# Moving the norm's roots to GpSimd's DMA queue and four reordering copies to ScalarE, in the first stage of a two-layer decoder trunk

## The chip, the cores and the metric

The kernel runs on one NeuronCore of a Trainium2 chip, in one launch. The metric is the device time of one execution in microseconds (us). A core has TensorE (PE: matmuls and transposes), VectorE (DVE), ScalarE (ACT), GpSimd (POOL) and SyncE (SP), each of which runs its own list of instructions in order. A DMA is an instruction of the engine on whose queue it is put (here SP or POOL); if it has to wait for its data or its buffer, everything behind it on that engine waits too.

## The reference

```python
h = x                                        # (1, 512, 1024) float32
# layer 0: dilated attention, 3 groups of 4 heads, then a gated FFN with a short convolution
g = norm_gains[0]
qkv = rms_norm(h, g[0]) @ w_qkv_a[0]         # rms_norm: x * rsqrt(mean(x*x) + eps) * gain
# group g of ((128,1), (512,4), (2048,16)): (window, dilation); rope on q and k;
# with dilation r the tokens are taken as t.reshape(L, r).T, so every r-th token is a sequence
...
h = h + rms_norm(mix, g[1])
h = h + rms_norm(conv_ffn(rms_norm(h, g[2]), ...), g[3])
# layer 1: forgetting attention with shared K/V, then the same kind of FFN
```

The change lies in the very first stage: the norm of x, its product with w_qkv_a, and the layout of the tokens for the dilated groups. The rest (about nine tenths of the time) is untouched.

## The kernel before

All products are done in three matmuls of split operands: a float32 array is held as a rounded high part and the remainder, the low part, and `mm3` (lines 287 to 290) adds high x high, high x low and low x high. So every activation and every weight must be split first: ScalarE writes the high part, VectorE subtracts to get the low part.

**Weights.** The class `Weights` (line 33) holds a list of pieces of 512 KB each, in the order of use. Its methods are called in the order in which the program text says so: `load` puts a piece's DMAs on SP's queue (line 48), `high` splits on ScalarE (line 62, with the norm's gain as scale), `low` on VectorE (line 80). `W.split(n)` splits all pieces up to n and loads a few pieces ahead of that; `W.get()` hands out the next pair and splits up to `W.ahead - 1` pieces beyond it. Pieces 0 to 3 are q and k of group 0, pieces 4 and 5 its v; 6 to 9 are q and k of group 1, 10 to 13 of group 2, 14 to 17 v of both. The first six pieces go into buffers called wearly, the later ones into wraw.

**The roots.** The norm's factor 1/sqrt(mean) is not applied to x. x is transposed and split as it is, and the factor is applied to each output row when a product leaves PSUM. `rstd0(b)` computes it for token block b (128 tokens): ScalarE squares and sums (1146), takes the root (1147), VectorE the reciprocal (1148), into `rt[:, 0, b]`. For the dilated groups the tokens are in another order, so the same 512 numbers are needed in that order: `factors_out` (1150) writes `rt[:, 0]` to a small DRAM tile `rd` (1151) and reads it back as `rt[:, 1]` (1152), both on SP's queue. The read-back waits for the write.

**The second token order.** `xT` holds the transposed x, in high and low part, each in two halves (i = 0, 1) of four 128-row chunks (kc 0 to 3 and 4 to 7). Groups 1 and 2 use a copy `xP`, in which the tokens stand as (r, l) instead of (l, r), with r = 4. `reorder` (1160) makes it: for each half, block and part one GpSimd copy of 128 x 512 (1167). Every block of 128 columns of `xP` holds tokens from all four blocks of `xT`.

**The order of the stage**, as written by hand from line 1375 on:

- q and k of group 0 for blocks 0 to 3 (`qk0`), with the transposes and splits of the blocks and the pieces between them. `qk_post` (1174) takes each result out of PSUM on ScalarE with the factor (1178), and applies the rope on GpSimd (1184 to 1187).
- After block 1's `qk_post`: `reorder(0, 1)` on GpSimd (8 copies), `rstd0(2)`, `rstd0(3)`, `factors_out()`.
- After block 3's: the first loads of `down_sums` for pair (1,6) on SP (576: it loads two chunks of a w_down, forms four sums on VectorE and writes them to DRAM for a later stage), then `reorder(2, 3)` (8 copies).
- `v_proj0` (1316): v of group 0. Its two `W.get()` split pieces 6 and 7, then 8, before anything else of it. Blocks 0 and 1 are computed, taken out on ScalarE (1331), and the list `between[0]` is run; then blocks 2 and 3 and `between[1]`. In those lists stand the transposes of q and k (`qk_transpose`: TensorE 1193, the copy out on VectorE 1196), the first scores and their softmax (TensorE 1218, VectorE 1203, ScalarE 1204), and steps of the down sums.
- `wide_proj(1, ...)` (1426): q and k of group 1 from `xP`, in four weight steps s of two chunks kc, over all four blocks in each step. Steps 0 and 1 read the half i = 0, steps 2 and 3 the half i = 1. In step 3 `qk_post(1, b)` applies `rt[:, 1]`. Then `wide_proj(2, ...)` in the same way, and v of groups 1 and 2.

Buffers come from pools with a fixed number of slots (16 large ones, 10 small ones, 8 PSUM banks); an allocation waits until the last user of a freed slot is done.

Of the kernel before, what the change touches and what calls it, by code (L numbers as in the profile page):

```python
# [9 lines left out]
F32 = mybir.dt.float32  # L10
# [105 lines left out]
def trunk_kernel(ctx, tc, x, norm_gains, w_qkv_a, w_o_a, w_q_b, w_o_b, kv_norm, w_kvf, b_f,  # L116
                 w_up, conv_w, conv_b, w_down, rope, out):
    nc = tc.nc
    act, dve, pool, pe, sp = nc.scalar, nc.vector, nc.gpsimd, nc.tensor, nc.sync
# [11 lines left out]
    def t4(shape, dt=F32, name="t4"):  # L131
        return p4.tile(shape, dt, tag="t4", name=name)
# [4 lines left out]
    def bank(shape, name="bank"):  # L137
        return psp.tile(shape, F32, tag="ps", name=name)
# [16 lines left out]
    for g in range(3):  # L155
        for s in range(4):
            def f(raw, g=g, s=s):
                v = raw.rearrange("p (k t c) -> p k t c", k=2, t=2)
                src = wqkv.rearrange("(k p) (t c) -> p k t c", p=128, c=256)
                return [(v[:, k], src[:, 2 * s + k, g:g + 4:3, :]) for k in range(2)]  # L160
# [126 lines left out]
    def mm3(o, ah, al, bh, bl, first, last, shared=False):  # L287
        pe.matmul(o, ah, bh, start=first, stop=False, skip_group_check=shared)  # L288
        pe.matmul(o, ah, bl, start=False, stop=False, skip_group_check=shared)  # L289
        pe.matmul(o, al, bh, start=False, stop=last, skip_group_check=shared)  # L290
# [285 lines left out]
    def down_sums(pairs, place, queue, lag, behind):  # L576


        live, n = [], len(pairs)
        for i in range(n + lag + behind):  # L580
            if i < n:
                l, j = pairs[i]
                a, b = place()
                live.append((a, b))
                r = w_down[l][j * 256:j * 256 + 256, :].rearrange("(c p) d -> c p d", p=128)
                sp.dma_start(a, r[0])
                sp.dma_start(b[:, 0:512], r[1, :, 512:1024])
                sp.dma_start(b[:, 512:1024], r[1, :, 0:512])
            if 0 <= i - lag < n:
                a, b = live[i - lag]  # L590
                dve.tensor_tensor(a[:, 0:512], a[:, 512:1024], a[:, 0:512], ALU.subtract)
                dve.tensor_tensor(a[:, 512:1024], b[:, 0:512], a[:, 512:1024], ALU.subtract)
                dve.tensor_tensor(b[:, 0:512], b[:, 0:512], a[:, 0:512], ALU.subtract)
                dve.tensor_tensor(b[:, 512:1024], b[:, 512:1024], b[:, 0:512], ALU.subtract)
            i -= lag + behind
            if i >= 0:
                l, j = pairs[i]
                for q, t in enumerate(live[i]):
                    queue.dma_start(dT[l][j, :, q * 1024:q * 1024 + 1024], t)
            yield  # L600
# [539 lines left out]
    rt = sml.tile([128, 2, 4], F32, tag="rt", name="rt", bufs=1)  # L1140
    rd = tc.dram_tile([T], F32, name="rd")

    def rstd0(b):
        ss, sd = small(1, "s1"), small(1, "sd")
        junk = t2([128, D], BF16, name="junk")
        act.activation(junk, h[:, b, :], AF.Square, scale=1.0 / 32, accum_out=ss)
        act.activation(sd, ss, AF.Sqrt, bias=eps_t)
        dve.reciprocal(rt[:, 0, b:b + 1], sd)

    def factors_out():  # L1150
        sp.dma_start(rd.rearrange("(b p) -> p b", p=128), rt[:, 0])
        sp.dma_start(rt[:, 1], rd.rearrange("(l r) -> l r", r=4))

    def factor(g, b):
        return rt[:, min(g, 1), b:b + 1]

    def by_fourth(a, spec="p k (l r) -> p k r l"):
        return a.rearrange(spec, r=4)

    def reorder(*blocks):  # L1160

        for i in range(2):
            for b in blocks:
                for part in range(2):
                    src = by_fourth(xT[part][i][:, :, b * 128:b * 128 + 128])
                    dst = xP[part][i].rearrange("p k (r l) -> p k r l", r=4)[:, :, :, b * 32:b * 32 + 32]
                    pool.tensor_copy(dst, src.bitcast(F32))

    def ax(g, b, kc):
        return xs(xP if g else xT, kc, slice(b * 128, b * 128 + 128))  # L1170
# [3 lines left out]
    def qk_post(g, b, o):  # L1174
        if b == 0:
            qks[g] = t8([128, 4, 8, HD], name=f"qk{g}")
        qk = qks[g][:, b]
        act.activation(qk.rearrange("p a d -> p (a d)"), o, AF.Identity, scale=factor(g, b))
        tu = t2([128, 2, 8, 16], name="tu")
        rb = 4 * min(g, 1) + b  # L1180
        c2 = rp[:, rb, None, 0:16].to_broadcast([128, 8, 16])
        s_lo = rp[:, rb, None, 16:24].to_broadcast([128, 8, 8])
        s_hi = rp[:, rb, None, 24:32].to_broadcast([128, 8, 8])
        pool.tensor_tensor(tu[:, 0], qk[:, :, 0:16], c2, ALU.mult)
        pool.tensor_tensor(tu[:, 1, :, 0:8], qk[:, :, 8:16], s_lo, ALU.mult)
        pool.tensor_tensor(tu[:, 1, :, 8:16], qk[:, :, 0:8], s_hi, ALU.mult)
        pool.tensor_tensor(qk[:, :, 0:16], tu[:, 0], tu[:, 1], ALU.add)
# [128 lines left out]
    def v_proj0(between):  # L1316
        banks = []
        ws = [[t.rearrange("p (k c) -> p k c", k=4) for t in W.get()] for _ in range(2)]
        for b in range(4):
            if b % 2 == 0:  # L1320
                banks.append(bank([128, 2, 256], name="v_ps"))
            for kc in range(KD):
                wh, wl = ws[kc // 4]
                ah, al = ax(0, b, kc)
                mm3(banks[b // 2][:, b % 2, :], ah, al, wh[:, kc % 4, :], wl[:, kc % 4, :],
                    kc == 0, kc == KD - 1)
            if b == 1:
                V[0] = t4([128, 4, 256], name="V0")
            if b % 2:
                for i in range(2):  # L1330
                    act.activation(V[0][:, b - 1 + i, :], banks[b // 2][:, i], AF.Identity, scale=factor(0, b - 1 + i))
                for f in between[b // 2]:
                    f()
# [4 lines left out]
    L = later  # L1338
# [68 lines left out]
                      same[:, None, :].to_broadcast([128, 32, 4]), ALU.add)  # L1407
    qk0(1, 6, 7)
    qk_post(0, 1, qk_banks[1])
    reorder(0, 1)  # L1410
    rstd0(2)
    rstd0(3)
    factors_out()
    qk0(2, *range(4))
    W.split(5)
# [5 lines left out]
    qk_post(0, 3, qk_banks[3])  # L1421
    sums = down_sums([(1, 6), (1, 7)], in_two, sp, 1, 3)
    next(sums)
    reorder(2, 3)

    def wide_proj(g, name, post, between):

# [15 lines left out]
    def v_post(g, b, o):  # L1443
        if b == 0:
            for i in (1, 2):
# [2 lines left out]
        dve.tensor_scalar(V[2][:, b, :], o[:, 256:512], factor(2, b), None, ALU.mult)  # L1448

    down0 = down_sums([*[(0, j) for j in range(ND)], (1, 8)], in_one, sp, 1, 1)  # L1450
    v_proj0([[L(qk_transpose, 0, 0), L(qk_transpose, 0, 1), L(next, down0)],
             [L(qk_transpose, 0, 2), L(qk_transpose, 0, 3), L(scores, 0, 0), L(scores, 0, 1), L(next, sums), L(next, down0)]])
    wide_proj(1, "qk_ps", qk_post, [
        [L(p_transpose, 0, 0)],
# [352 lines left out]
    for n in range(N + 3):  # L1807
        live = n < N
        if live:
            j, i = units[n]  # L1810
# [93 lines left out]
```

## Time and profile before

| | us |
|---|---|
| median of 3 runs (lowest, highest) | 1109.35 (1109.13, 1109.38) |
| the profiled execution, its own time | 1110.01 |
| span of the profiled execution, first to last instruction | 1108.2 |
| TensorE busy / mean granted clock | 1095.6 (99%) / 0.996 |
| VectorE, ScalarE, GpSimd busy | 895.7, 730.9, 234.8 |
| DMA moved | 252.06 MB, 227 GB/s on average |

The profile shows one execution, instruction by instruction. In a timeline each row gives the start and length in us, the engine, the line of the kernel, the operation with its tiles (output <- inputs), and in brackets how long the engine stood idle before it and which instruction, or which DMA, ended that idle time. Rows with "q" after the engine's name (SPq) are DMA instructions on that engine's queue; their length is the issue and not the transfer. A list of waits sums such idle time by waiter and releaser. TensorE's granted clock is given as a share of full speed.

The stage of the change takes about the first 140 us. From 0 to 20 us TensorE is busy for 17.68 us, from 20 to 40 for 20.00, from 40 to 60 for 16.42 at a mean clock of 0.83, and from then on nearly without a gap at 1.00. The DMA engines' share is 0.80 in the first 20 us, 0.15 from 20 to 40, and about 1 from there to 120.

### The profile page before, as it was taken

What the parts mean: (1) busy time and instruction counts of PE and PEld (TensorE: products, weight loads), DVE (VectorE), ACT (ScalarE), POOL (GpSimd) and SP (SyncE); (2) the same over time, 40 slices, a digit from 0 to 9 for tenths busy, and PEclk for the clock granted to TensorE, in tenths of its full rate; (3) what the DMA queues carried; (4) which work ended last, traced back from release to release, by engine and by line L of the source; (5) the groups of instructions that cost most, each with busy time, mean ns of one, the idle gap of its engine ahead of it and who ended that gap; (6) DMA issues with size and microseconds to landing.
All of it is one profiled execution on the core that took longest, in us unless ns stands there. A gap on an engine that the chain in (4) does not pass through costs nothing. (4 is left out here: it accounts for less than half of the span.)

```text
span 1108.2 us, 18988 instructions
## 1 busy us (share of the span) xinstructions
PE 1095.6 (99%) x6905; PEld 970.1 (88%) x6905; DVE 895.7 (81%) x1453; ACT 730.9 (66%) x1228; POOL 234.8 (21%) x337
## 2 busy tenths in 40 slices
PE   9899999999999999999999999999999999999997
PEld 6788888999999988888878888888999999988886
DVE  5797788977887789997598777878977887789994
ACT  6454566677878757576563488846677878757572
POOL 2713100422222111000000545600422222211000
PEclk9899999999999999999999999999999999999999
DMA  5699963499999998884446756783499999999862
GB/s 195 243 354 404 367 194 99 96 228 228 235 223 238 225 297 314 324 314 123 133 152 232 244 153 158 224 269 97 96 227 233 236 217 245 222 296 315 321 247 76
DMA packets 156614, 252.06 MB, mean 227 GB/s; under 512 B 12960, under 2 KB 99992, under 8 KB 156520
## 3 DMA queue, kind: packets, MB, share of 16 engines
q1 hardware_dynamic: 138248, 186.61, 50.5%
q0 software_dynamic: 18272, 64.24, 26.2%
q8 instruction: 54, 0.88, 0.3%
q14 instruction: 40, 0.33, 0.1%
HBM read 166.08 MB, written 39.63 MB: 186 GB/s over the span
## 5 line engine op out<-in xcount | busy, mean ns | idle before, releaser
L288 PE MATMUL up<-xsh,w 128*128 128x256 f32 x512 | 144.9, 283 | 0.0
L289 PE MATMUL up<-xsl,w 128*128 128x256 f32 x512 | 144.9, 283 | 0.0
L290 PE MATMUL up<-xsh,w 128*128 128x256 f32 x512 | 144.9, 283 | 0.0
L288 PE MATMUL acc<-w 128*128 128x512 f32 (+1 forms) x311 | 120.7, 388 | 0.3 <-DVE mix L337 0.3
L290 PE MATMUL acc<-w 128*128 128x512 f32 (+1 forms) x311 | 120.6, 388 | 0.1
L705 ACT CAST w<-wraw 128x1024 fp32r<-128x1024 f32 x80 | 82.6, 1048 | 37.7 <-DVE wraw L689 37.7
L624 DVE SCALAR_TENSOR_TENSOR bb<-up,conv,bb 128x511 f32<-128x511 f32 x80 | 59.8, 747 | 57.2 <-ACT bb L623 57.0
L289 PE MATMUL acc<-w 128*128 128x512 f32 (+1 forms) x267 | 103.3, 387 | 0.0
L288 PEld LDWEIGHTS up<-xsh,w 128*128 128x128 f32 x512 | 98.3, 192 | 0.0
L289 PEld LDWEIGHTS up<-xsl,w 128*128 128x128 f32 x512 | 98.3, 192 | 0.0
L290 PEld LDWEIGHTS up<-xsh,w 128*128 128x128 f32 x512 | 98.3, 192 | 0.0
L623 ACT ACTIVATE bb<-up,conv 128x512 f32<-128x512 f32 x80 | 60.1, 778 | 32.7 <-DVE up L775 24.4
L288 PE MATMUL up<-xch,w 128*128 128x256 f32 (+1 forms) x256 | 80.0, 312 | 0.1
L288 PE MATMUL up<-xbh,w 128*128 128x256 f32 (+1 forms) x256 | 80.0, 312 | 0.1
L708 POOL DMA_DIRECT2D w<-wraw x48 | 41.0, 853 | 181.6 <-ACT w L707 102.9
L289 PE MATMUL up<-xcl,w 128*128 128x256 f32 (+1 forms) x256 | 79.2, 310 | 0.0
L289 PE MATMUL up<-xbl,w 128*128 128x256 f32 (+1 forms) x256 | 79.2, 310 | 0.0
L290 PE MATMUL up<-xbh,w 128*128 128x256 f32 (+1 forms) x256 | 79.2, 309 | 0.0
L290 PE MATMUL up<-xch,w 128*128 128x256 f32 (+1 forms) x256 | 79.2, 309 | 0.0
L76 DVE TENSOR_TENSOR w<-wraw,w 128x1024 fp32r<-128x1024 f32 x48 | 65.0, 1378 | 11.7 <-ACT w L58 11.2
L58 ACT CAST w<-wraw 128x1024 fp32r<-128x1024 f32 x62 | 63.8, 1052 | 15.6 <-PE v_ps L289 6.9
L290 PEld LDWEIGHTS acc<-w 128*128 128x128 f32 x311 | 58.4, 188 | 12.7 <-DVE w L817 0.9
(304 smaller groups left out, 3283.7 us busy)
## 6 DMA issues: line engine op xcount, KB each, us to landing
wraw<-in_w_up_dram SPq DMA_DIRECT2D x88, 512.0 KB, 7.0
w<-wraw POOLq DMA_DIRECT2D x62, 512.0 KB, 7.7
dT<-dsums SPq DMA_DIRECT2D x28, 512.0 KB, 6.9
dsums<-in_w_down_dram SPq DMA_DIRECT2D x22, 512.0 KB, 7.7
dsums<-in_w_down_dram SPq DMA_DIRECT2D x44, 256.0 KB, 6.9
hD<-hc POOLq DMA_DIRECT2D x44, 256.0 KB, 7.3
wraw<-dT SPq DMA_DIRECT2D x22, 512.0 KB, 7.0
dact<-hD SPq DMA_DIRECT2D x44, 256.0 KB, 5.4
```

The costliest lines, as they stand in the source:

```text
L58: self.nc.scalar.copy(pair[:, 0], raw)
L76: self.nc.vector.tensor_tensor(pair[:, 1], raw, pair[:, 0].bitcast(F32), ALU.subtract)
L288: pe.matmul(o, ah, bh, start=first, stop=False, skip_group_check=shared)
L289: pe.matmul(o, ah, bl, start=False, stop=False, skip_group_check=shared)
L290: pe.matmul(o, al, bh, start=False, stop=last, skip_group_check=shared)
L623: act.activation(bb[:, s, :], ps, AF.Identity, bias=cp[:, 3, ch:ch + 1], scale=cp[:, 2, ch:ch + 1])
L624: dve.scalar_tensor_tensor(bb[:, s, 1:], ps[:, :T - 1], cp[:, 1, ch:ch + 1], bb[:, s, 1:], ALU.mult, ALU.add)
L705: act.copy(w[:, 0], self.f[key])
L708: pool.dma_start(w[:, 1], self.f[key], accum_op=ALU.add)
```

## The change

Two things are changed. The write of the roots to DRAM and their read-back go from SP's queue to GpSimd's; the write stays at its place in the program, behind `reorder` of blocks 0 and 1, and the read-back becomes a function of its own, `factors_in`, called after the second `reorder`. And that second `reorder`, of blocks 2 and 3, is cut in two: GpSimd makes the four copies of the half i = 0 as before, and ScalarE makes the four of the half i = 1, at the head of `between[0]` of `v_proj0`, behind the V copies of blocks 0 and 1.

```diff
     def factors_out():
-        sp.dma_start(rd.rearrange("(b p) -> p b", p=128), rt[:, 0])
-        sp.dma_start(rt[:, 1], rd.rearrange("(l r) -> l r", r=4))
+        pool.dma_start(rd.rearrange("(b p) -> p b", p=128), rt[:, 0])
+
+    def factors_in():
+        pool.dma_start(rt[:, 1], rd.rearrange("(l r) -> l r", r=4))
...
-    def reorder(*blocks):
+    def reorder(blocks, halves, copy):
 
-        for i in range(2):
+        for i in halves:
             for b in blocks:
                 for part in range(2):
...
-                    pool.tensor_copy(dst, src.bitcast(F32))
+                    copy(dst, src.bitcast(F32))
...
     qk_post(0, 1, qk_banks[1])
-    reorder(0, 1)
+    reorder((0, 1), (0, 1), pool.tensor_copy)
     rstd0(2)
     rstd0(3)
     factors_out()
...
     next(sums)
-    reorder(2, 3)
+    reorder((2, 3), (0,), pool.tensor_copy)
+    factors_in()
...
-    v_proj0([[L(qk_transpose, 0, 0), L(qk_transpose, 0, 1), L(next, down0)],
+    v_proj0([[L(reorder, (2, 3), (1,), act.copy), L(qk_transpose, 0, 0), L(qk_transpose, 0, 1), L(next, down0)],
              [L(qk_transpose, 0, 2), L(qk_transpose, 0, 3), L(scores, 0, 0), L(scores, 0, 1), L(next, sums), L(next, down0)]])
```

No arithmetic is changed; the copies have the same operands on either engine.

## The prediction

> **What bounds the kernel now.** I read the page first, then the list of waits, then the timelines of the first 110 us, engine by engine. TensorE is busy nearly always, so only its few gaps and its clock can be won. The page's busy line, and two rows of TensorE's waits over the whole run (waiter, releaser: total us, times, longest):
>
> ```profile
> PE 1095.6 (99%) x6905; PEld 970.1 (88%) x6905; DVE 895.7 (81%) x1453; ACT 730.9 (66%) x1228; POOL 234.8 (21%) x337
> PE s_ps L1218 <- DVE qkT L1196: 3.6, 1, 3.6
> PE pT_ps L1240 <- DVE st L1203: 0.2, 1, 0.2
> ```
>
> One gap of 3.6 us stands out, before the first scores of group 0 (L1218), which need the transposed block that VectorE copies out in L1196. It lies inside the stage that the change touches. TensorE's timeline there (start, length, instruction, idle before it):
>
> ```profile
> 38.43 1.03 PE L1193 MATMUL qkT_ps<-ident,qk 128*128 128x128 f32 x8
> 45.05 1.04 PE L1193 MATMUL qkT_ps<-ident,qk 128*128 128x128 f32 x8
> 49.67 3.10 PE L1218 MATMUL s_ps<-qkT 64*128 64x128 f32 x16 [3.58 <-DVE qkT L1196]
> 52.70 0.79 PE L288 MATMUL qk_ps<-w,xph 128*128 128x512 f32 x1
> 59.55 0.60 PE L1240 MATMUL pT_ps<-ident,p 128*128 128x128 f32 x4
> 59.90 0.48 PE L288 MATMUL qk_ps<-w,xph 128*128 128x512 f32 x1
> 65.56 2.10 PE L1218 MATMUL s_ps<-qkT 64*128 64x256 f32 x16
> 67.65 0.52 PE L1240 MATMUL pT_ps<-ident,p 128*128 128x128 f32 x3
> 107.34 1.26 PE L1220 MATMUL s_ps<-qkT 64*128 64x128 f32 x16
> 108.54 0.66 PE L1240 MATMUL pT_ps<-ident,p 128*128 128x128 f32 x4
> ```
>
> The gap also costs clock. In the view by windows, columns are the window, its length, then busy us of PE, PEld, DVE, ACT and POOL, granted clock, DMA share, GB/s:
>
> ```profile
> 24.00:34.00 10.00, 10.00 (x52) 8.48 (x51) 8.47 (x9) 5.96 (x14) 9.93 (x9) 1.00 0.03 0
> 46.00:48.00 2.00, 0.09 (x1) 0.00 (x0) 1.09 (x1) 1.85 (x4) 1.80 (x2) 1.00 1.10 360
> 50.00:52.00 2.00, 2.00 (x15) 2.00 (x14) 2.00 (x10) 0.65 (x3) 0.00 (x0) 0.50 1.03 389
> 54.00:56.00 2.00, 2.00 (x7) 1.52 (x7) 1.93 (x5) 2.00 (x8) 0.00 (x0) 0.64 1.02 376
> ```
>
> The clock is full until 48, half after the gap, and full again in the course of 54 to 56 (0.64 over 2 us is half for 1.44, so until 55.4). The first of these rows matters next: from 24 to 34 the DMA engines moved nothing.
>
> Why VectorE was late: it copies qkT (48.94) only after splitting weight pieces 6, 7 and 8 (L80), which waited for ScalarE's halves (L62), which waited for DMA.
>
> ```profile
> 25.85 9.11 DVE L80 SCALAR_TENSOR_TENSOR w<-wearly,gcol,w 128x256 fp32r<-128x256 f32 x8 [0.24 <-ACT w L62]
> 40.07 5.74 DVE L80 SCALAR_TENSOR_TENSOR w<-wraw,gcol,w 128x512 fp32r<-128x512 f32 x4 [5.10 <-ACT w L62]
> 46.91 2.11 DVE L80 SCALAR_TENSOR_TENSOR w<-wraw,gcol,w 128x512 fp32r<-128x512 f32 x2 [1.11 <-ACT w L62]
> 48.94 2.47 DVE L1196 COPY qkT<-qkT_ps 128x512 f32<-128x512 f32 x4
> ...
> 32.88 0.69 ACT L1178 ACTIVATE qk<-qk_ps,rt 128x512 f32<-128x512 f32 x1 [3.16 <-PE qk_ps L290]
> 39.31 2.94 ACT L62 ACTIVATE w<-wraw,gcol 128x512 fp32r<-128x512 f32 x4 [5.74 <-DMA wraw<-in_w_qkv_a_dram]
> 46.15 1.39 ACT L62 ACTIVATE w<-wraw,gcol 128x512 fp32r<-128x512 f32 x2 [3.91 <-DMA wraw<-in_w_qkv_a_dram]
> 47.45 1.55 ACT L1331 ACTIVATE V<-v_ps,rt 128x256 f32<-128x256 f32 x4
> ```
>
> And why those pieces came late, from SP's timeline, SP's list of waits and the DMA issues (count, KB each, us to landing):
>
> ```profile
> 9.84 1.13 SPq L48 DMA_DIRECT2D wearly<-in_w_qkv_a_dram  x2
> 34.50 1.96 SPq L48 DMA_DIRECT2D wraw<-in_w_qkv_a_dram  x4
> 38.27 4.92 SPq L48 DMA_DIRECT2D wraw<-in_w_qkv_a_dram  x6
> ...
> SPq L1151 <- DVE rt L1148: 14.3, 1, 14.3
> SPq L1152 <- DMA rd<-rt: 8.0, 1, 8.0
> ...
> wraw<-in_w_qkv_a_dram SPq DMA_DIRECT2D x12, 256.0 KB, 7.3
> ```
>
> SP stood for 14.3 us until the last root was there, then for 8.0 us until its write had landed; pieces 6 and 7 went out at 34.50, right behind, with no wait of their own.
>
> **The change part by part.** *The roots leave SP's queue.* Two DMAs go; behind them SP has pieces 6 and 7 (four DMAs), three loads of down pair (1,6), and pieces 8 to 10 (six). Up to there buffers are still in first use or already free, so these issue from about 11.3 (after 9.84 + 1.13) and, at the lengths of 34.50 and 38.27, are out by about 20. With 7.3 us to landing all is there by some 28, in DMA time that now lies empty; the first loads stand ahead of them in the same queue.
>
> *ScalarE* is then free for L62 at 32.88 + 0.69 = 33.6: pieces 6 and 7 take 2.94, piece 8 takes 1.39, done at 37.9. The first V copies (half of 1.55) follow when TensorE has finished the second block, 38.43, and end at 39.2. The *four new copies* come next. No row shows them; bounds for 128x512 are a plain L62 (1.39 / 2 = 0.70) and a strided copy, L1297 below, 1.14. I take 1.14, as the order is strided: 4.6 us, 39.2 to 43.8 (below: 42.0). What is queued behind them, V of blocks 2 and 3, is due only when TensorE ends them at 45.05. Idle time of ScalarE (42.25 to 46.15 before) hides them; if they ran past 45.05, V's bank and the exponentials would slip first. Their target, half i=1, is read only in the third of the four weight steps, some 12 us after the first.
>
> *VectorE* ends pieces 4 and 5 at 34.96, then has six L80. They take 0.74 each undisturbed and 5.74 / 4 = 1.43 beside GpSimd's copies, so 4.4 to 8.6: end 39.4 to 43.6. Two qkT copies of 2.47 / 4 = 0.62: 40.6 to 44.8. TensorE comes to the scores at 45.05 + 1.04 = 46.09. The stall goes, with 1.3 us to spare at the worst.
>
> ```profile
> 34.05 0.64 POOL L1184 TENSOR_TENSOR tu<-qk,rope 128x128 f32<-128x128 f32 x1
> 37.42 1.12 POOL L1167 CAST xph<-xah 128x512 fp32r<-128x512 f32 x1
> 46.70 1.10 POOL L1167 CAST xpl<-xal 128x512 fp32r<-128x512 f32 x1
> L648 POOL DMA_DIRECT2D hD<-hc x42: 539/886/904, 221.1 to 1004.2; - x42
> L1297 ACT COPY ow<-o_ps x4: 1094/1138/1176, 143.1 to 147.1; 128x512 f32<-128x512 f32 x4
> ```
>
> *GpSimd* is next late, if anything. At 34.05 it now issues the write of the roots. L648 (min, median, max ns) costs 0.89 for 128 runs; this write is 512 runs of 4 bytes: 0.54 to 4 x 0.89 = 3.5; I take 0.9, the nearest row. Queued behind it are the rope of blocks 2 and 3 (34.05 to 37.42, 3.4) and now only four copies at (46.70 + 1.10 - 37.42) / 8 = 1.30, that is 5.2 instead of 10.4. End: 34.05 + 0.9 + 3.4 + 5.2 = 43.5. With 3.5 for the DMA and every L80 (six of 0.74) held in front of it: 34.05 + 3.5 + 3.4 + 5.2 + 4.4 = 50.5. TensorE needs these halves at 47.7 (below). So 0, with up to 2.8 us for the range. Then the read-back waits on GpSimd for the write (8.0 before); nothing follows there until the rope of group 1, near 78, and ScalarE wants the factors only at 77.13:
>
> ```profile
> 77.13 0.69 ACT L1178 ACTIVATE qk<-qk_ps,rt 128x512 f32<-128x512 f32 x1
> 105.96 2.42 ACT L1178 ACTIVATE qk<-qk_ps,rt 128x512 f32<-128x512 f32 x4 [2.15 <-DMA dT<-dsums]
> ```
>
> At 43.5 + 8.0 + 7.3 = 59 it is there, even against 77.13 - 6.2. Cost nothing.
>
> **The sum.** The stall: 3.58. The half clock: the first scores, half of them narrow, took 52.70 - 49.67 = 3.03; at full clock a group of wide ones takes 67.65 - 65.56 = 2.09 and of narrow ones 108.54 - 107.34 = 1.20, half of each 1.64, so 1.39 lost (and the halves are needed at 46.09 + 1.64 = 47.7). The first 24 matmuls of the wide projection took 59.55 - 52.70 = 6.85, the next 24 took 65.56 - 59.90 = 5.66: 1.19 lost. Together 3.58 + 1.39 + 1.19 = 6.2. The profiled execution took 1110.01 (span 1108.2 and 1.8 around it); it becomes 1103.8. The runs' median, 1109.35, is 0.66 below it and would become 1103.15, say 1103.2.
>
> The Trainium skill, "TensorE: Matmul & The Clock Gate", Part 1, says that an idle window of about 3.4 us halves the clock and a busy one of about 3.4 us restores it, on a free-running window. The trace agrees with the halving; by the page half speed would last 3.4 us and cost 1.7, an estimate, for a gain of 5.3. The rows show half clock from 49.67 to 55.4, which decides.
>
> **The rivals.** *A part is given back (17%).* Two places: GpSimd's halves end after 47.7 (up to 2.8 us, too short to be like the gap that halved the clock), or the down sums hold TensorE. For the second speaks the row at 105.96: ScalarE waited 2.15 us there for a buffer that a DMA of the sums empties, and the DMA engines are full from 34 on. TensorE's next bank (108.95, after 108.54) is cleared at 105.96 + 0.6, so 2.4 us of slack; if these transfers did not move at all, TensorE would lose 6.2 - 2.4 = 3.8. Against it: 3.5 MB of them leave some 20 us earlier. So 1104.4 to 1107.0.
>
> *Nothing moves (7%).* SP's queue is not what held the loads, or freeing it saves only two issues; about 1109.3. The Trainium skill, "DMA: Bandwidth & Descriptors", "Issuing engines are not separate DMA queues", says that issuing from another engine saves only the sequencer's time for the issue, which would be no more than SP's own instructions here. Against this rival stand the 14.3 and 8.0 us in SP's list: it is the waiting in front of an issue that leaves with it.
>
> *Slower (6%).* GpSimd pays per 4-byte run and the write holds it long. Rope and copies would then end at 43.5 - 0.9 + T. TensorE's first wide matmul was at 52.70; with T = 10.1 it starts where it did, and beyond that each us is lost. With T = 15 it starts at 57.6, 4.9 later: 1114.3. Against it: L648 would have to be exceeded seventeen times.
>
> **How the numbers follow.** Full gain 70%: from 1102.3 (all 5.7 us at half clock lost by half, 2.9, and the 0.66 between profile and median not there) to 1104.4 (only the scores' 1.39 won beside the gap). The range takes this and most of the partial case: 1102.3 to 1106.2. About 0.2% (2.2 us) is what a measurement can tell; faster by more than that are both first cases, 87%; same 7%; slower 6%.
>
> **What would show it.** Right: no wait of TensorE for L1196; clock 1.00 from 46 to 56; loads of pieces 6 and 7 from 11.3; L62 at 33.6; the first L288 with xph near 47.7 instead of 52.70; GpSimd's last copy near 43.5. Wrong: a new wait of TensorE for GpSimd's copies at 47.7, a long GpSimd DMA at 34.05, ScalarE's wait at L1178 grown beyond 2.15 us with TensorE waiting behind it, or L62 still waiting for wraw.

## The result and the profile after

| | before | after |
|---|---|---|
| median, us (lowest, highest, runs) | 1109.13 (1108.41, 1109.38, 5) | 1104.31 (1103.36, 1104.93, 6) |
| profiled execution, its own time | 1110.01 | 1104.32 |
| span / mean granted clock | 1108.2 / 0.996 | 1102.5 / 0.998 |

The ratio of the times is 0.9956, 95% interval 0.9943 to 0.9970: 4.9 us faster (3.3 to 6.3). Forecast were 6.2 us and 1103.2. (Two runs of the kernel before, 2783.97 and 1338.73 us, and one of the fourth experiment, 2156.86 us, lie far above all others and aren't counted.)

In the changed kernel the lines behind the edit are 2 or 3 higher: L1196 of before is L1198, L1218 is L1220. The page's busy line, with TensorE 2.0 us less busy (that is clock: the matmuls are the same 6905), and TensorE's waits over the whole run:

```profile
PE 1093.6 (99%) x6905; PEld 968.5 (88%) x6905; DVE 892.3 (81%) x1453; ACT 735.1 (67%) x1232; POOL 231.5 (21%) x335
```

```profile
PE warm L248 <- DVE zero L243: 1.2, 1, 1.2
PE qk_ps L289 <- DVE w L80: 0.3, 1, 0.3
PE acc L288 <- DVE mix L337: 0.3, 1, 0.3
PE pT_ps L1242 <- DVE st L1205: 0.2, 1, 0.2
```

The wait of 3.6 us for the qkT copy is gone and nothing has taken its place. TensorE's timeline in the stage:

```profile
38.88 1.04 PE L1195 MATMUL qkT_ps<-ident,qk 128*128 128x128 f32 x8
45.50 1.03 PE L1195 MATMUL qkT_ps<-ident,qk 128*128 128x128 f32 x8
46.47 1.68 PE L1220 MATMUL s_ps<-qkT 64*128 64x128 f32 x16
48.08 0.50 PE L288 MATMUL qk_ps<-w,xph 128*128 128x512 f32 x1
53.66 0.60 PE L1242 MATMUL pT_ps<-ident,p 128*128 128x128 f32 x4
```

The scores follow the transposes at once and take 1.68 us instead of 3.10; the first wide matmul comes at 48.08 instead of 52.70. Below, a *stretch* means the time from the second group of qkT transposes to the first pT transpose, that is from 45.50 to 53.66 here: 8.16 us. Before it was 45.05 to 59.55, 14.50. (The opening differs by 0.4 us, 38.88 against 38.43 for the first transposes, and did so at the first matmul already, before any moved load was issued; further executions of before lie between 38.38 and 38.91. The stretch is free of that.) The windows (PE, PEld, DVE, ACT, POOL busy, clock, DMA share, GB/s):

```profile
24.00:34.00 10.00, 10.00 (x49) 8.40 (x49) 8.03 (x9) 6.35 (x17) 9.92 (x11) 1.00 0.41 132
46.00:48.00 2.00, 2.00 (x21) 1.58 (x19) 1.86 (x9) 1.97 (x4) 0.34 (x1) 1.00 0.34 82
50.00:52.00 2.00, 2.00 (x10) 1.65 (x9) 1.90 (x4) 2.00 (x7) 0.00 (x0) 1.00 1.09 368
```

The clock stays at 1.00, and the DMA engines, which stood still from 24 to 34 before (share 0.03), now finish the moved loads there (0.41). And the chain of causes behind it, in the timelines of SP, ScalarE, VectorE and GpSimd in turn:

```profile
10.08 1.11 SPq L48 DMA_DIRECT2D wearly<-in_w_qkv_a_dram  x2
11.53 3.85 SPq L48 DMA_DIRECT2D wraw<-in_w_qkv_a_dram  x4
19.04 4.63 SPq L48 DMA_DIRECT2D wraw<-in_w_qkv_a_dram  x6
...
33.92 3.78 ACT L62 ACTIVATE w<-wraw,gcol 128x512 fp32r<-128x512 f32 x6
39.08 0.84 ACT L1333 ACTIVATE V<-v_ps,rt 128x256 f32<-128x256 f32 x2 [1.38 <-PE v_ps L290]
39.81 1.12 ACT L1169 CAST xph<-xah 128x512 fp32r<-128x512 f32 x1
42.93 1.15 ACT L1169 CAST xpl<-xal 128x512 fp32r<-128x512 f32 x1
...
35.32 5.06 DVE L80 SCALAR_TENSOR_TENSOR w<-wraw,gcol,w 128x512 fp32r<-128x512 f32 x6
40.30 1.27 DVE L1198 COPY qkT<-qkT_ps 128x512 f32<-128x512 f32 x2
...
34.45 0.95 POOL L1151 DMA_DIRECT2D rd<-rt  x1
37.44 0.79 POOL L1189 TENSOR_TENSOR qk<-tu 128x128 f32<-128x128 f32 x1
40.63 0.46 POOL L1189 TENSOR_TENSOR qk<-tu 128x128 f32<-128x128 f32 x1
41.04 1.13 POOL L1169 CAST xph<-xah 128x512 fp32r<-128x512 f32 x1
44.28 1.14 POOL L1169 CAST xpl<-xal 128x512 fp32r<-128x512 f32 x1
45.76 0.58 POOL L1154 DMA_DIRECT2D rt<-rd  x1 [0.34 <-DMA rd<-rt]
```

Read from the top: pieces 6 and 7 go out at 11.53 instead of 34.50; ScalarE splits them and piece 8 from 33.92 on with no wait (5.74 and 3.91 us of waits before), VectorE follows at 35.32, and the first qkT copy is made at 40.30 instead of 48.94, with TensorE not there before 46.47.

### The profile page after: what moved, and what is told of

It reads as the page before. It is cut to its first block, busy times and chain, and to the rows that moved or that the text cites. A ratio compares the mean times of both kernels' runs of the same rounds, so it can differ in the third digit from the quotient of the medians.

```text
span 1102.5 us, 18986 instructions
## 1 busy us (share of the span) xinstructions
PE 1093.6 (99%) x6905; PEld 968.5 (88%) x6905; DVE 892.3 (81%) x1453; ACT 735.1 (67%) x1232; POOL 231.5 (21%) x335
## 4 chain that ended last, share of the span: by engine, by line
PE 85%; issue 9%; DVE 2%; ACT 2%; DMA 1%; POOL 1%; DVEq 0%; SPq 0%; POOLq 0%; ACTq 0%
PE up L288 12%; PE up L289 12%; PE up L290 12%; PE acc L288 8%; PE acc L290 8%; PE acc L289 8%; PE qk_ps L289 2%; PE qk_ps L288 2%; PE qk_ps L290 2%; PE s_ps L1733 2%; PE o_ps L1781 2%; PE pT_ps L1766 1%; PE first L290 1%; PE first L288 1%; PE first L289 1%
## 5 line engine op out<-in xcount | busy, mean ns | idle before, releaser
L705 ACT CAST w<-wraw 128x1024 fp32r<-128x1024 f32 x80 | 82.6, 1048 | 37.7 <-DVE wraw L689 37.7
```

The lines of the kernel that those rows point to most:

```text
L705: act.copy(w[:, 0], self.f[key])
```

## The experiments

Theory 1, that of the prediction: the loads of pieces 6 to 8 had stood behind two waits on SP, and whatever takes these waits from in front of them wins the gap and the clock lost with it. Rivals: GpSimd's lighter load (four copies instead of eight) wins a part; the clock loss is a cost of its own; only a second queue helps. Each timed kernel had runs of the kernel before beside it on the same chip: median 1109.22 us (1107.69 to 1110.49, 27 runs) for experiments 1, 2, 3 and 7, 1109.29 (1108.70 to 1110.84, 8 runs) for 4, 5 and 6.

**1. The queue alone.** Against the changed kernel:

```diff
-    reorder((2, 3), (0,), pool.tensor_copy)
+    reorder((2, 3), (0, 1), pool.tensor_copy)
...
-    v_proj0([[L(reorder, (2, 3), (1,), act.copy), L(qk_transpose, 0, 0), L(qk_transpose, 0, 1), L(next, down0)],
+    v_proj0([[L(qk_transpose, 0, 0), L(qk_transpose, 0, 1), L(next, down0)],
```

> Only the roots' two DMAs go to GpSimd's queue; all eight copies of blocks 2 and 3 stay on GpSimd, the read-back behind them. Theory 1 (SP's wait held the weight loads, and that made VectorE late): the whole gain, as the half i = 0 is still made first: no wait of TensorE for L1196, first wide matmul near 48.1, about 1104.3 us, within 0.7 of the changed kernel. Theory 2 (GpSimd's copies beside VectorE's splits made VectorE late, so the four copies on ScalarE carry the gain): the gap stays for the most part, 1107 to 1109.

Measured: 1103.96 us (1103.52 to 1104.00), ratio 0.9952 (0.9939 to 0.9964). Its timelines of TensorE and GpSimd:

```profile
46.36 1.68 PE L1220 MATMUL s_ps<-qkT 64*128 64x128 f32 x16
...
44.17 1.14 POOL L1169 CAST xpl<-xal 128x512 fp32r<-128x512 f32 x1
48.44 1.13 POOL L1169 CAST xpl<-xal 128x512 fp32r<-128x512 f32 x1
```

Its stretch is 8.16 us, as with the whole change. GpSimd's eight copies end at 49.57, but the half i = 0 is done at 45.31, ahead of the first wide matmul (47.97), and the other half isn't read before the third weight step. The queue carries the whole gain.

**2. The copies alone.** Against the changed kernel: both DMAs on SP at their old place.

```diff
     def factors_out():
-        pool.dma_start(rd.rearrange("(b p) -> p b", p=128), rt[:, 0])
+        sp.dma_start(rd.rearrange("(b p) -> p b", p=128), rt[:, 0])
...
-        pool.dma_start(rt[:, 1], rd.rearrange("(l r) -> l r", r=4))
+        sp.dma_start(rt[:, 1], rd.rearrange("(l r) -> l r", r=4))
...
     factors_out()
+    factors_in()
...
     reorder((2, 3), (0,), pool.tensor_copy)
-    factors_in()
```

> Only the four copies of the half i = 1 go to ScalarE; the roots' write and read-back stay on SP's queue at their old place. Theory 1: pieces 6 to 8 are as late as before, the gap stays at 3 to 3.6 us (at most 0.5 less, as the last two L80 run undisturbed), half clock behind it: 1108.5 to 1109.3 us. Theory 2: the gap goes, near 1104.3.

Measured: 1108.44 us (1107.63 to 1109.50), ratio 0.9993 (0.9984 to 1.0002). Its timelines of TensorE, ScalarE and VectorE:

```profile
48.94 3.09 PE L1220 MATMUL s_ps<-qkT 64*128 64x128 f32 x16 [2.57 <-DVE qkT L1198]
...
46.08 1.41 ACT L62 ACTIVATE w<-wraw,gcol 128x512 fp32r<-128x512 f32 x2 [4.20 <-DMA wraw<-in_w_qkv_a_dram]
...
46.84 1.45 DVE L80 SCALAR_TENSOR_TENSOR w<-wraw,gcol,w 128x512 fp32r<-128x512 f32 x2 [2.54 <-ACT w L62]
```

ScalarE still waits for piece 8. With GpSimd's last copies gone, VectorE's last two L80 take 1.45 instead of 2.11 us and follow ScalarE more closely, so the gap is 2.6 instead of 3.6 us; in the time this can hardly be told from nothing.

**3. The write on SP, the read-back on GpSimd.** Only the second of SP's waits, the 8.0 us for the write to land, is meant to leave SP; the copies are as in the change.

```diff
     def factors_out():
-        pool.dma_start(rd.rearrange("(b p) -> p b", p=128), rt[:, 0])
+        sp.dma_start(rd.rearrange("(b p) -> p b", p=128), rt[:, 0])
```

> The change with the write of the roots back on SP's queue at its old place, the read-back on GpSimd's. SP then waits for the last root (14.3 us before) but not for the write to land (8.0). Theory 1: pieces 6 and 7 leave near 26 instead of 11.5 or 34.5, land near 33.4, just when ScalarE is free (33.6), piece 8 near 37: the whole gain, 1104.3 us; so the 8.0 us alone carried the loss. If the load time itself counts, part of the gap comes back: 1105.5 to 1107. If the early loads made the opening 0.4 us later in the changed kernel, this one is 0.4 faster than it: 1103.9, first matmul at 7.0 instead of 7.4.

Measured: 1105.72 us (1105.08 to 1107.73), ratio 0.9973 (0.9964 to 0.9982). I had expected the full gain; about a third of it was missing (3.5 us came, 5.3 in the first run). TensorE's waits, SP's timeline with one of its waits, and the windows of this kernel (its profiled execution took 1107.01, one of the slower ones):

```profile
PE s_ps L1220 <- DVE qkT L1198: 1.9, 1, 1.9
PE qk_ps L288 <- ACT V L1333: 0.7, 1, 0.7
```

```profile
25.86 0.37 SPq L1151 DMA_DIRECT2D rd<-rt  x1
26.27 2.04 SPq L48 DMA_DIRECT2D wraw<-in_w_qkv_a_dram  x4
...
SPq L48 <- DMA rd<-rt: 4.8, 1, 4.8
```

```profile
28.00:30.00 2.00, 2.00 (x11) 1.65 (x10) 2.00 (x3) 1.94 (x5) 2.00 (x3) 1.00 0.02 6
34.00:36.00 2.00, 2.00 (x19) 2.00 (x18) 1.19 (x2) 0.00 (x0) 1.92 (x5) 1.00 0.21 20
38.00:40.00 2.00, 2.00 (x20) 2.00 (x20) 1.10 (x2) 1.49 (x3) 2.00 (x2) 1.00 1.08 393
```

The loads of pieces 6 and 7 were issued at 26.27, right behind the write, with nothing on SP in between. But the DMA engines moved 6 to 48 GB/s from 28 to 36 us and full speed only from 38 on. So SP's order isn't all: the write itself held what stood behind it in the queue. And SP was not rid of its wait: it stood another 4.8 us for the same write in front of the next weight load, the eighth DMA behind it, so that the loads from piece 8 on went out only from 35.02 (why SP waits there isn't shown). Piece 8 is what ScalarE waited for last, until 46.06, so TensorE's 1.9 us can't be put down to the queue alone. The late weights also moved V and ScalarE's four copies (47.40 to 51.58) into each other's way, which is the wait of 0.7 us.

**4. The same with longer runs.** Against the third kernel, the write goes out as 128 runs of 16 bytes instead of 512 of 4; the reordering is left to the read-back, in four DMAs on GpSimd.

```diff
-        sp.dma_start(rd.rearrange("(b p) -> p b", p=128), rt[:, 0])
+        sp.dma_start(rd.rearrange("(p b) -> p b", b=4), rt[:, 0])
...
-        pool.dma_start(rt[:, 1], rd.rearrange("(l r) -> l r", r=4))
+        for b in range(4):
+            pool.dma_start(rt[b * 32:b * 32 + 32, 1], rd.rearrange("(l r b) -> l r b", r=4, b=4)[:, :, b])
```

> As the run with the write on SP at its old place, but the write goes out as 128 runs of 16 bytes instead of 512 runs of 4, and GpSimd reads it back with four DMAs of 128 runs of 4. Theory 1 (the many 4-byte runs of the write are what held the loads behind it): the write lands in 2 to 3 us, pieces 6 and 7 are there by about 34, the wait of TensorE for the qkT copy is under 0.3 and the time is 1104.3. Rival (any write to DRAM in front of the loads holds the queue, whatever its runs, or the loads issued at 26.3 are simply too late): the wait stays at 1.9, the time at 1105.7.

Measured: 1104.00 us (1103.65 to 1104.07), ratio 0.9948 (0.9934 to 0.9962), stretch 8.17. Windows and TensorE's timeline:

```profile
28.00:30.00 2.00, 2.00 (x11) 1.65 (x10) 2.00 (x3) 1.70 (x5) 2.00 (x2) 1.00 0.48 107
30.00:32.00 2.00, 2.00 (x11) 1.65 (x10) 2.00 (x3) 0.00 (x0) 2.00 (x3) 1.00 1.10 386
```

```profile
46.00 1.68 PE L1221 MATMUL s_ps<-qkT 64*128 64x128 f32 x16
```

With the loads issued at 26.02, nearly the same moment, full speed comes at 30 instead of 38, SP doesn't wait for the write (piece 8's loads go out from 29.71), and the gap is gone. So it was the form of the write, 512 runs of 4 bytes, that held the queue. Whether the number of runs or their size counts, the two kernels don't tell apart.

**5. Both DMAs on SP, behind the loads.** The copies are as in the change; no DMA of the roots is on GpSimd's queue.

```diff
-        pool.dma_start(rd.rearrange("(b p) -> p b", p=128), rt[:, 0])
+        sp.dma_start(rd.rearrange("(b p) -> p b", p=128), rt[:, 0])
...
-        pool.dma_start(rt[:, 1], rd.rearrange("(l r) -> l r", r=4))
+        sp.dma_start(rt[:, 1], rd.rearrange("(l r) -> l r", r=4))
...
-    factors_out()
...
-    factors_in()
...
-    v_proj0([[L(reorder, (2, 3), (1,), act.copy), L(qk_transpose, 0, 0), L(qk_transpose, 0, 1), L(next, down0)],
+    v_proj0([[factors_out, factors_in, L(reorder, (2, 3), (1,), act.copy), L(qk_transpose, 0, 0), L(qk_transpose, 0, 1), L(next, down0)],
```

> Both DMAs of the roots stay on SP, but behind the ten loads of the weight pieces and the down pair instead of ahead of them; GpSimd issues neither, and the copies are as in the change. Theory 1 (what counts is that no load stands behind the roots' write, whichever queue carries it): no wait of TensorE for L1198's copy, L62 of pieces 6 and 7 at 33.9, first wide matmul near 48.1, time 1104.3 (1103.5 to 1105). Rival (GpSimd's queue itself is what helps, because two queues move more than one): the wait stays in part and the time is 1105.5 or more. A third outcome: the write, about 8 us in flight, holds the down-sum loads that now stand behind it; the first of them is issued at about 33.3 in the changed kernel, so it would slip by a few us at most, and ScalarE's wait at L1180 near 100 would grow without TensorE waiting.

Measured: 1103.78 us (1103.56 to 1104.58), ratio 0.9948 (0.9935 to 0.9961), stretch 8.16. SP's timeline:

```profile
11.20 3.84 SPq L48 DMA_DIRECT2D wraw<-in_w_qkv_a_dram  x4
...
25.86 0.37 SPq L1151 DMA_DIRECT2D rd<-rt  x1
34.25 0.34 SPq L1154 DMA_DIRECT2D rt<-rd  x1
34.69 1.30 SPq L586 DMA_DIRECT2D dsums<-in_w_down_dram  x1
```

SP waits as long for the write to land as before (7.9 us), but all loads that are due are out by then. The next one goes out at 34.69 instead of 33.32, which costs nothing. No second queue is needed; what counts is which loads stand behind the roots.

**6. GpSimd's slack.** The queue change with all eight copies on GpSimd, but the half i = 1 first, so that the half that is needed first ends last.

```diff
-    reorder((2, 3), (0,), pool.tensor_copy)
+    reorder((2, 3), (1, 0), pool.tensor_copy)
...
-    v_proj0([[L(reorder, (2, 3), (1,), act.copy), L(qk_transpose, 0, 0), L(qk_transpose, 0, 1), L(next, down0)],
+    v_proj0([[L(qk_transpose, 0, 0), L(qk_transpose, 0, 1), L(next, down0)],
```

> The queue part of the change with all eight copies of blocks 2 and 3 on GpSimd, but half i=1 first, so that the half that the first wide matmuls read ends last, at about 49.5 instead of 44.2. Theory 1 (GpSimd had 3.7 us of slack for the first half, and behind that TensorE waits): TensorE waits 1.5 us at the first wide matmul (47.97 before), the clock stays at 1.00, since the wait is shorter than the one that halved it, and the time is 1105.5. Rival (the wait costs clock as well, like the 3.6 us one): 1106.5 to 1107.5. If there is no wait, the copies' order carries nothing and the time is 1104.0.

Measured: 1105.18 us (1104.91 to 1106.76), ratio 0.9965 (0.9950 to 0.9979); the fifth kernel, on the same chip, took 1103.56 to 1104.58. TensorE's timeline:

```profile
48.52 0.50 PE L288 MATMUL qk_ps<-w,xph 128*128 128x512 f32 x1 [0.51 <-POOL xph L1169]
```

GpSimd's last copy ended at 49.51. TensorE waited 0.5 us for the last high part and 0.3 for the last low part, and the stretch grew from 8.16 to 9.33 at full clock. So the rival of the prediction, GpSimd late, is real; in the change it just isn't reached.

**7. The gap filled.** The kernel before with 15 more matmuls, whose result is not used, in front of the first scores. It leaves everything late, but keeps TensorE busy.

```diff
+    def keep_warm(n):
+        o = bank([128, 512], name="warm")
+        for i in range(n):
+            pe.matmul(o, xT[0][0][:, 0, 0:128], xT[0][0][:, 0, :], start=True, stop=True)
...
-             [L(qk_transpose, 0, 2), L(qk_transpose, 0, 3), L(scores, 0, 0), L(scores, 0, 1), L(next, sums), L(next, down0)]])
+             [L(qk_transpose, 0, 2), L(qk_transpose, 0, 3), L(keep_warm, 15), L(scores, 0, 0), L(scores, 0, 1), L(next, sums), L(next, down0)]])
```

> The kernel before with 15 extra matmuls (results unused, 0.2275 us each, 3.4 us in all) in TensorE's gap ahead of the first scores. Theory 1: the idle time stays lost, but the clock stays full: a gain of the clock's part alone, 2.6 us, to 1106.7 us. If half the clock cost nothing beside the gap: 1109.3.

Measured: 1108.19 us (1107.66 to 1109.33), ratio 0.9992 (0.9984 to 1.0001). The profiled execution took 1107.66, that is 2.35 less than that of before, with the clock at 1.00 throughout:

```profile
46.01 3.67 PE L249 MATMUL warm<-xah 128*128 128x512 f32 x15
49.71 1.74 PE L1223 MATMUL s_ps<-qkT 64*128 64x128 f32 x16
```

In the profile the clock's part is nearly the 2.6 us of the prediction; in the medians it is 1.0 (-0.1 to 1.8 by the interval), and the 1106.7 that I had expected was missed. The stretch is 11.76 us, 2.74 less than in the first execution of before. One fixed loss of clock doesn't fit both, which led to the last runs.

**8. The same two kernels again.** Three more profiled executions of before, two more of after, nothing edited.

> The kernel before, unchanged, profiled once more, to see how much of its gap and of its clock loss repeats from execution to execution. Theory 1 (the gap of 3.6 us is fixed by the order of the work, but the throttle's window runs free of it, so the stretch at half clock differs between executions): gap 3.4 to 3.7, clock between 48 and 56 different from 0.61, 0.50, 0.50, 0.69, span between 1105.3 and 1108.2. Rival (both repeat): the same windows, span 1107.7 to 1108.3, and the 0.8 us between 5.7 in the profiles and 4.9 in the medians stays unexplained.

> The kernel before, unchanged, a third profiled execution. In the first the clock was halved behind the gap of 3.58 us (0.61, 0.50, 0.50, 0.69 in the four windows from 48 to 56), in the second it stayed at 1.00 behind a gap of 3.42 us. Theory 1 (the throttle's window runs free, so a gap of about 3.5 us is at its limit and halves the clock in some executions only): either is possible, the gap is 3.4 to 3.7 in each, and the end of the first weight step, 59.55 and 57.33 before, is near one of the two. Rival (the second execution was an exception): half clock again, end near 59.5.

> The kernel before, unchanged, a fourth profiled execution, for the same question and with the same expectations as the third: by theory 1 the half clock is there in some of the four and missing in others, by the rival it is missing in the second alone.

> The changed kernel, unchanged, a second profiled execution. By theory 1 it has no gap in which the clock could be halved, so it repeats closely: no wait of TensorE for L1198, clock 1.00 from 46 to 56, span 1102.0 to 1102.8 (1102.5 in the first). Rival (the clock is lost here too in some executions): half clock in this stretch, span 1104 or more.

> The changed kernel, unchanged, a third profiled execution, with the same expectations as the second: clock 1.00 from 46 to 56 and span 1102.0 to 1102.8, or, by the rival, half clock in this stretch and 1104 or more.

The second execution of before (timeline, then a window):

```profile
49.98 1.83 PE L1218 MATMUL s_ps<-qkT 64*128 64x128 f32 x16 [3.42 <-DVE qkT L1196]
```

```profile
50.00:52.00 2.00, 2.00 (x17) 1.54 (x18) 2.00 (x6) 0.50 (x2) 0.00 (x0) 1.00 1.04 391
```

The third (the fourth is like it, with 0.91, 0.50 and 0.74 in these windows):

```profile
48.00:50.00 2.00, 0.52 (x6) 0.52 (x8) 2.00 (x4) 1.88 (x3) 0.27 (x1) 0.92 1.05 396
50.00:52.00 2.00, 2.00 (x14) 1.71 (x12) 2.00 (x11) 0.54 (x3) 0.00 (x0) 0.50 1.03 388
52.00:54.00 2.00, 2.00 (x9) 1.36 (x7) 1.64 (x11) 2.00 (x10) 0.00 (x0) 0.73 1.04 400
```

A clock of c over 2 us is half clock for 4 x (1 - c) us. The first execution's half clock begins in a row that the prediction doesn't show:

```profile
48.00:50.00 2.00, 0.33 (x2) 0.33 (x4) 2.00 (x4) 1.98 (x4) 0.00 (x0) 0.66 1.04 393
```

So, with the windows of the four executions added up:

| execution | gap | at half clock | stretch | more than 8.16 |
|---|---|---|---|---|
| before, first (the prediction's) | 3.58 | 1.36 + 2.0 + 2.0 + 1.44 = 6.8 | 14.50 | 6.34 |
| before, second | 3.42 | 0 | 11.80 | 3.64 |
| before, third | 3.44 | 0.32 + 2.0 + 1.08 = 3.4 | 13.27 | 5.11 |
| before, fourth | 3.42 | 0.36 + 2.0 + 1.04 = 3.4 | 13.16 | 5.00 |
| after, all three | none | 0 | 8.16 each | 0 |

The gap repeats; the half clock comes in none, one or two pieces of 3.4 us. The second has the stretch of the kernel with the filled gap (11.80 and 11.76). In the first the half clock begins at 48.64, before the gap ends at 49.67, so part of its 6.8 us fell on idle time. The mean of the last column is 5.02, and 4.9 was timed; with four executions between 3.64 and 6.34, so close an agreement is partly luck. The timed runs agree that the loss comes and goes: of the 35 counted runs of before beside the experiments, the 7 with a mean granted clock of 0.996 or less took 1110.2 us on average, the 12 with 0.998 or more 1109.0, while all runs of the first and the fifth kernel had 0.998 or 0.999. (The own times of single executions don't show this: the second took 1108.90, the third 1108.66, the fourth 1108.98. The second came to the first cq_ps transpose 0.6 and 0.8 us ahead of these two, at 590.9, and had lost that lead by 730 us, far from the change.)

## Why the prediction was right, and where its size was off

*The mechanism* was right at every step that the time hangs on. The loads went out at 11.53 (11.3 forecast), L62 began at 33.92 (33.6) and was done at 37.7 (37.9), the first wide matmul came at 48.08 (47.7, plus the 0.4 of the opening). The loads were out at 23.7 and not by 20, as they took longer to issue than in before (3.85 us for the first four, 1.96 there); that cost nothing, for the DMA engines were idle again by 30 and ScalarE came to them at 33.92.

*VectorE's six L80* took 5.06 us (4.4 to 8.6 forecast), *ScalarE's copies* 1.12 to 1.15 each (1.14), from 39.81 to 44.08, ahead of V at 45.70.

*GpSimd's last copy* ended at 45.4, not 43.5. The write's issue was right (0.95 for 0.9), the copies were shorter (4.4 for 5.2), but the rope took from 35.41 to 41.09, 5.7 instead of the 3.4 of before: it now ran beside VectorE's L80, which the change had moved forward, and one L1189 took 0.79 there and 0.46 once they were done. I had costed the copies by their disturbed length and the rope, which took their place beside L80, by a mostly undisturbed one. The Trainium skill, "GPSIMD Engine Reference", Section 1, says that GpSimd's SBUF interfaces are shared with VectorE, with contention when VectorE has two SBUF inputs; L80 has two, and the rows agree. TensorE needed the half at 48.08, so 2.7 us of slack were left, and the sixth run shows what lies beyond.

*The rivals.* The down sums took nothing: ScalarE's wait at that place grew from 2.15 to 2.75 us, and TensorE doesn't wait there.

```profile
100.71 2.42 ACT L1180 ACTIVATE qk<-qk_ps,rt 128x512 f32<-128x512 f32 x4 [2.75 <-DMA dT<-dsums]
```

"Nothing moves" fell: what left with the two DMAs was the waiting in front of the loads. The rule behind it, from the Trainium skill, "DMA: Bandwidth & Descriptors", "Issuing engines are not separate DMA queues", that issuing from another engine saves only the time of the issue, doesn't count such waiting. The fifth run agrees with it that the second queue as such gave nothing: it is as fast on SP's queue alone. "Slower", by a long issue of the write on GpSimd, fell with 0.95 us. It was nearer the truth than I thought in one point: the 4-byte runs are dear, but on SP's DMA queue (third run), not on GpSimd, which issues them here. Whether loads behind the write on GpSimd's queue would have been late as in the third run was not tried. The prediction also took a wait of 2.8 us as too short to halve the clock; in the second run a gap of 2.57 us was followed by half clock.

*The size.* 4.9 us came, 6.2 were forecast. The term that failed is the half clock, 1.39 + 1.19 = 2.58, and the step is the sentence that weighed the Trainium skill, "TensorE: Matmul & The Clock Gate", Part 1, against one profiled execution: "The rows show half clock from 49.67 to 55.4, which decides." They decided for that execution alone, the one with two pieces of half clock. Over four executions the stretch lost 0, 1.36, 1.47 and 2.70 us beyond the 3.64 of the second, 1.4 in the mean, and 3.64 + 1.4 = 5.0. The same part of the Trainium skill says that the window is about 3.4 us long and free-running, and that the loss at a kernel's start therefore differs from run to run. The four executions agree, behind a gap too: half clock came in pieces of about 3.4 us, and 5.3, the estimate from one such window, was closer than 6.2. The profiled execution agrees too: with the row from 48 to 50 its half clock is 6.8 us, two windows, and not the 5.7 that the prediction read from 49.67 on. The second half of the mistake was to carry the full gain over to the median, though the median stood 0.66 below the profiled execution: that difference may have been a sign of the same thing, since a median with less clock loss has less to win back. The seventh run had shown it first, with 2.35 in the profile and 1.0 in the medians.

*What the change's two parts are worth.* The queue: all of it. The copies on ScalarE: nothing on top (first run), about one us of gap without it (second run), where the ratio is uncertain by as much. The simplest version is the first kernel; the fifth, with the two DMAs moved behind the loads on SP, needs no second queue (it was run with the four copies on ScalarE only). Both are as fast as the change within their intervals (0.9952, 0.9948, 0.9956), and none is shown to be faster.

What stays open: the third kernel's runs lie in two clumps, 1105.1 to 1105.7 (six of them) and 1106.8 to 1107.7 (five), and its profiled execution is of the upper one, with the clock at 1.00 through its gaps. Probably the hold of the queue differs from run to run; that was not traced. Nor is it known why the second execution of before lost its lead far from the change.

## What to carry to other kernels

Before moving work off an engine, look at what waits *in front* of a late load in the same queue: here, putting a DMA that waits behind the loads that don't wait was worth as much as another engine, and cost nothing. A loss of clock behind a gap should be priced over several executions, and not by the one that was profiled. When a change moves one engine's work forward, reprice what it will then run beside.

## What the runs showed of the hardware that was not expected

A write of 2 KB to DRAM in 512 runs of 4 bytes held the loads behind it in SP's queue for about 8 us: 6 to 48 GB/s from 28 to 36 us, 393 from 38. In 128 runs of 16 bytes it let them pass at 386 GB/s from 30. On GpSimd's queue, where no load stood behind it, the first form took 11.0 us from issue to landing, with other transfers beside it (0.37 + 8.0 = 8.4 on SP's in the kernel before, on idle DMA engines), and TensorE waited for nothing behind it.

Behind the same gap of 3.4 to 3.6 us the clock was halved for 0, 3.4, 3.4 and 6.8 us in four executions. The gap of 2.57 us in the second run went with 6.8 us at half clock (0.61, 0.50, 0.50 and 0.69 in the windows from 48 to 56), that of 1.92 us in the third by none. So a gap of 2.6 us is not safe; one execution each doesn't show where safety begins.
